# Low-order halves of some weight splits moved 32 bytes off a multiple of 64

## The chip, the cores and the metric

The kernel runs on one core of a Trainium2 chip. The metric is the device time of one execution in microseconds (us). TensorE does the matmuls, VectorE (DVE in the profile) and ScalarE (ACT) prepare weights and evacuate results, GpSimd (POOL) does small work and issues some DMAs, SyncE (SP) issues the weight DMAs. SBUF is the on-chip memory: 128 partitions, and an address in this text is a byte offset within a partition. PSUM holds the matmuls' sums.

## What is computed

A two-layer backbone over 256 latent tokens and 256 context tokens, width 1024. Each layer is an FFN, a mixing step with 16 attention heads of three kinds, and a second FFN, all pre-normed and modulated:

```python
for l in range(DEPTH):
    h = h + 0.5 * g1 * _swiglu(_modulate(_rms_norm(h, norm_ffn1[l]), sh1, sc1),
                               w_ffn1_gate[l], w_ffn1_up[l], w_ffn1_down[l])
    hc = hc + 0.5 * cg1 * _swiglu(...)              # same weights, context tokens
    p = u @ w_in[l]                                 # q, k, v of all heads
    ...
    h = h + gm * (jnp.concatenate([y_w, y_g, y_n], axis=-1) @ w_out[l])
    if not last: hc = hc + cgm * (yc @ w_out[l])
    h = h + 0.5 * g2 * _swiglu(...)
    if not last: hc = hc + 0.5 * cg2 * _swiglu(...)
```

The FFN's inner width is 2816. In the last layer the context tokens are needed only as keys and values, so its queries, output projection and second FFN run on the 256 latent tokens alone.

## The kernel before

Activations lie transposed: 128 channels on the partitions, 512 token columns (0 to 255 latent, 256 to 511 context). Weights come in chunks of 128 x 1024, one DMA each, into a `raw` buffer (three of them). To keep precision, each operand of a large matmul is split into a high part in the reduced type float32r and a low part that holds the rest: `wload` (L126) lets ACT copy the raw chunk to the high part (L129) and VectorE subtract it from the raw chunk for the low part (L130). Both parts lie in one `split` tile of 2 x 1024 elements, of which there are four buffers, 8192 bytes each: high part first, low part 4096 bytes on. The activations are split likewise (`Uh`, `Ul`, and `G` for the FFN's hidden tiles).

A product is then three matmuls per 128 x 128 weight block, in `mm3` (L133): high weight by high activation (L134), high weight by low activation (L135), low weight by high activation (L136). Each matmul instruction has its own weight load in the program that runs (PEld in the profile). A weight load reads 128 elements, 512 bytes per partition.

How many columns a matmul streams depends on the place. Where latent and context tokens run together it is 512. It is 256

- in the whole second FFN of layer 1 and in the queries and the output projection of layer 1 (latent tokens only);
- in the last of the four parts of `down` in each FFN and in the second part of the output projection, where latent and context tokens go one after the other, so that the next norm can begin (`piece`, `finish`);
- in the first two tiles of the second FFN of layer 0 and of the first of layer 1 (`up_two`), and in the first key and query chunks of a mixer, which also run per token half.

The order of the work around this is set by the program's order and the tile scheduler. `MIX` is a hand-written order of the mixer's steps, `START` one of the first tiles; neither is touched. A one-off tile named `fill` of 288 bytes stands ahead of the weight pool. With it, in the built program, `raw`, `split`, `H`, `Uh`, `Ul` and the `G` tiles all begin at multiples of 512 bytes: the four `split` buffers at 44544, 52736, 60928 and 69120.

Of the kernel before, what the change touches and what calls it, by code (L numbers as in the profile page):

```python
# [10 lines left out]
F32 = mybir.dt.float32  # L11
F32R = mybir.dt.float32r
AF = mybir.ActivationFunctionType
ALU = mybir.AluOpType
# [46 lines left out]
def hybrid_backbone(ctx: ExitStack, tc: tile.TileContext, I, out):  # L61
# [61 lines left out]
        nc.sync.dma_start(raw[:, :n], src)  # L123
        return raw

    def wload(src, n=1024):  # L126
        raw = raw_load(src, n)
        sp = wp.tile([128, 2, 1024], F32R, tag="split", name="split", bufs=4)
        act(sp[:, 0, :n], raw[:, :n], AF.Copy)  # L129
        tt(sp[:, 1, :n], raw[:, :n], sp[:, 0, :n].bitcast(F32), ALU.subtract)  # L130
        return sp

    def mm3(ps, wh, wl, xh, xl, first, last):  # L133
        mm(ps, wh, xh, start=first, stop=False)  # L134
# [3 lines left out]
    def proj(ps, sp, U, cols, nk=KT, off=0, k0=0, ks=None):  # L138
        for k in ks or range(nk):
            o = off + k * 128  # L140
            mm3(ps, sp[:, 0, o:o + 128], sp[:, 1, o:o + 128], U[0][:, k0 + k, cols], U[1][:, k0 + k, cols],
                k == 0, k == nk - 1)


# [116 lines left out]
    def first_tiles(pool, csel, U, src):  # L261

        pss, sps, rb, ada_ps, ada_pt, rstd, tmp = [], [], [], {}, {}, {}, {}

        def r(h):
            if not rb:
                rb.append(bank("o", "rb"))
            rstd[h] = norm_rstd_stages(h, rb[0], 256 * h, "mm")  # L270
            next(rstd[h])

        def s(h):
            next(rstd[h], None)

        def a(p, i):

            if i == 0:
                ada_ps[p] = bank("mm", "adaps")
            c, b = divmod(i, 2)  # L280
            raw = pool.tile([128, 4, 256], F32, tag="araw", name="araw", bufs=ABUFS)
            nc.sync.dma_start(raw, I["w_ada0"][:, p, c, b])
            for j in range(4):
                mm(ada_ps[p][32 * j:32 * j + 32, :256], csel[:, 2 * j + b, c, :], raw[:, j, :], start=(i == 0),
                   stop=(i == 3))

        def b(p):
            sb = pool.tile([128, 256], F32, tag="adasb", name="adasb", bufs=1)
            act(sb, ada_ps[p][:, :256], AF.Copy)
            pt = ada_pt[p] = bank("mm", "adapt")  # L290
            for i in range(2):
                nc.tensor.transpose(pt[:, i * 128:(i + 1) * 128], sb[:, i * 128:(i + 1) * 128], ident)

        def c(p):
            v = ada_pt[p][:, :256].rearrange("p (b j r) -> p b r j", b=2, j=4)
            for i in range(2):
                f = i * KT + 2 * p
                nc.vector.tensor_reduce(ada[0][:, f:f + 2, :], v[:, :, 2 * i:2 * i + 2, :], axis=AX.X, op=ALU.add)
            for m in ("sh1", "sc1"):
                ada_fin(0, m, 2, slice(2 * p, 2 * p + 2))  # L300

        def w(i):
            raw = raw_load(src(i), 1024)
            if i < 4:
                t = wp.tile([128, 2, 1024], F32R, tag="split", name="split", bufs=4)
                parts = [(t, 0, 1024)]
            else:
                parts = [(pool.tile([128, 2, 512], F32R, tag="G", name="split0", bufs=10), o, 512) for o in (0, 512)]
            for t, o, n in parts:
                act(t[:, 0, :], raw[:, o:o + n], AF.Copy)  # L310
            sps.append((raw, parts))

        def x(i):
            raw, parts = sps[i]
            for t, o, n in parts:
                tt(t[:, 1, :], raw[:, o:o + n], t[:, 0, :].bitcast(F32), ALU.subtract)
            pss.append(bank(("s", "t", "s", "t", "mm", "mm")[i], "pf"))

        def u(f):
            shv = mod(0, "sh1")  # L320
            t2 = pool.tile([128, 2, TOK], F32R, tag="G", name="t0", bufs=10)[:, 0, :].bitcast(F32)
            for h in range(2):
                cols = (LAT, CT)[h]
                t = tmp[f, h] = t2[:, cols]
                stt(t, H[:, f, cols], amod[0][:, 0, f, h:h + 1], rb[0][:, 256 * h:256 * h + 256], op0=ALU.mult,
                    op1=ALU.mult)
                marks["act"] = ins_of(act(U[0][:, f, cols], t, AF.Identity, bias=shv[:, f, h:h + 1]))

        def v(f):
            shv = mod(0, "sh1")  # L330
            for h in range(2):
                cols = (LAT, CT)[h]
                stt(U[1][:, f, cols], tmp.pop((f, h)), shv[:, f, h:h + 1], U[0][:, f, cols].bitcast(F32),
                    op0=ALU.add, op1=ALU.subtract)

        def m(i, f):
            t, o, _ = sps[i][1][f // 4 if i >= 4 else 0]
            wh, wl = (t[:, e, f * 128 - o:f * 128 - o + 128] for e in range(2))
            mm(pss[i], wh, U[0][:, f, :], start=(f == 0), stop=False)
            mm(pss[i], wl, U[0][:, f, :], start=False, stop=False)  # L340
            mm(pss[i], wh, U[1][:, f, :], start=False, stop=(f == KT - 1))

        steps = dict(r=r, s=s, a=a, b=b, c=c, w=w, x=x, u=u, v=v, m=m)
        with tc.manual_schedule():
            for o in START.split():
                steps[o[0]](*map(int, o[1:]))
        return pss


    def ffn(l, w, halves, pool, U, jobs, after, start=None):  # L350
# [12 lines left out]
                done += 1  # L363

        def chunk(src, ft):
            return wload(src[l, :, ft * 1024:(ft + 1) * 1024])

        def evac(pg, pu):
            g = pool.tile([128, 2, TOK], F32R, tag="G", name="G", bufs=10)
# [28 lines left out]
        def down(p0, n, last):  # L398
            if not last:
                for d in range(KT):  # L400
                    sp = wload(wd[l, :, off[0]:off[0] + n * 128], n * 128)
                    off[0] += n * 128
                    ps = bank("mm", "pd")
                    for k in range(n):
                        mm3(ps[:, cols], sp[:, 0, k * 128:k * 128 + 128], sp[:, 1, k * 128:k * 128 + 128],
                            G[p0 + k][:, 0, cols], G[p0 + k][:, 1, cols], k == 0, k == n - 1)
                    for h in halves:
                        accum(ps, h * 256, d, h, gate)
            else:
                sps = []  # L410
                for i in range(KT // 2):
                    sps.append(wload(wd[l, :, off[0]:off[0] + n * 256], n * 256))
                    off[0] += n * 256
                def piece(ps, d, h):
                    c = (LAT, CT)[h]
                    o = (d % 2) * n * 128
                    for k in range(n):
                        mm3(ps[:, :256], sps[d // 2][:, 0, o + k * 128:o + k * 128 + 128],
                            sps[d // 2][:, 1, o + k * 128:o + k * 128 + 128],
                            G[p0 + k][:, 0, c], G[p0 + k][:, 1, c], k == 0, k == n - 1)  # L420

                finish(halves, piece, gate, after)
# [30 lines left out]
    def mixer(l, pool, U):  # L453
# [5 lines left out]
            late[n] for n in ("perm", "rope", "maskA", "maskC", "hsel", "qkg", "sink", "nsink", "qg8"))  # L459

        def qk_chunk(i):
            return wload(win[l, :, i * 1024:(i + 1) * 1024])

        def rope_lat(x):
            sw = bank("mm", "sw")
# [109 lines left out]
        def v_tok(sps, nk, n, dst, t):  # L575
            ps = bank("mm", "pv")
            for k in range(KT):
                s, o = sps[k // nk], (k % nk) * n
                c = slice(t * 128, t * 128 + 128)
                mm(ps[:, :n], U[0][:, k, c], s[:, 0, o:o + n], start=(k == 0), stop=False)  # L580
                mm(ps[:, :n], U[0][:, k, c], s[:, 1, o:o + n], start=False, stop=False)
                mm(ps[:, :n], U[1][:, k, c], s[:, 0, o:o + n], start=False, stop=(k == KT - 1))
            p = ps[:, :n].rearrange("p (h d) -> p h d", d=64)
            act(dst[:, t, :, 0, :], p, AF.Copy)
            tt(dst[:, t, :, 1, :], p, dst[:, t, :, 0, :].bitcast(F32), ALU.subtract)
# [185 lines left out]
    def out_proj(l, halves, Y, qcols, after):  # L771
# [5 lines left out]
        for part in range(2):  # L777
            sps = []
            if part == 0:
                for d in range(KT):  # L780
                    if d % 2 == 0:
                        i = d // 2
                        sp = wload(I["w_out"][l, :, i * 1024:(i + 1) * 1024])
                    ps = bank("mm", "pd")
                    proj(ps[:, qcols], sp, Z, qcols, nk=4, off=(d % 2) * 512)
                    for h in halves:
                        accum(ps, h * 256, d, h, gate)
            else:
                sps = [wload(I["w_out"][l, :, (4 + i) * 1024:(5 + i) * 1024]) for i in range(4)]

                def piece(ps, d, h):
                    proj(ps[:, :256], sps[d // 2], Z, (LAT, CT)[h], nk=4, off=(d % 2) * 512, k0=4)

                finish(halves, piece, gate, after)
# [154 lines left out]
```

## Time and profile before

| what | us |
|---|---|
| median of three runs (1742.02 to 1744.09) | 1743.22 |
| the profiled execution's own time | 1742.45 |
| its span, first to last instruction | 1740.5 |
| TensorE (PE) busy, 9572 matmuls | 1700.8 |
| VectorE (DVE) busy | 1180.0 |
| ScalarE (ACT) busy | 718.5 |

The profiled execution is one run; its span leaves out 1.95 us at its ends. An engine's busy time is the union of its instructions. A matmul's recorded length contains its passage through the array, which overlaps the next matmul, so the distance between starts, not the length, is what a matmul costs in a dense stream.

### The profile page before, as it was taken

The page shows a single profiled execution, that of the slowest core. Times are in us where ns is not written, and L with a number is a line of the kernel's source. Part 1 is how long each engine was busy: PE and PEld are TensorE (multiplying, and loading weights), DVE is VectorE, ACT ScalarE, POOL GpSimd, SP SyncE. Part 2 cuts the span into 40 slices and gives each one's busy share as a digit, 9 for nine tenths or more (in the row PEclk, how much of TensorE's full clock was granted, in tenths as well). Part 3 has the DMA queues.
Part 4 walks back from the last instruction along what each step waited for, and adds up shares of the span by engine and source line. Part 5 has one row for each costly group of instructions (what it writes and reads, how often), then busy time and mean ns, then how long its engine had stood idle before and what let it go on. Part 6 is the DMA issues. An engine that isn't in the chain of part 4 may idle for free.

```text
span 1740.5 us, 24756 instructions
## 1 busy us (share of the span) xinstructions
PE 1700.8 (98%) x9572; PEld 1477.5 (85%) x9572; DVE 1180.0 (68%) x2031; ACT 718.5 (41%) x1206; POOL 165.8 (10%) x251
## 2 busy tenths in 40 slices
PE   7999999999999999999999999999999999989997
PEld 4888888889888898888888898888888888889997
DVE  5899963447978869983334599934343787965555
ACT  4322222235888653222222442222222577754443
POOL 0311100012102031100000212100000211100000
PEclk9999999999999999999999999999999999989999
DMA  8877643323223247743333288824332333356663
GB/s 330 309 240 243 197 117 84 110 73 115 58 82 85 75 169 238 236 129 89 108 85 109 63 319 277 321 79 115 85 109 86 99 84 102 109 155 182 182 176 113
DMA packets 76693, 258.37 MB, mean 148 GB/s; under 512 B 8944, under 2 KB 11248, under 8 KB 76192
## 3 DMA queue, kind: packets, MB, share of 16 engines
q1 hardware_dynamic: 54096, 176.72, 33.2%
q0 software_dynamic: 21760, 79.38, 14.3%
q8 instruction: 75, 1.23, 0.3%
q10 hardware_dynamic: 720, 0.69, 0.1%
q14 instruction: 42, 0.34, 0.1%
HBM read 250.47 MB, written 1.05 MB: 145 GB/s over the span
## 4 chain that ended last, share of the span: by engine, by line
PE 89%; DVE 4%; ACT 4%; issue 2%; POOL 1%; DMA 1%; POOLq 0%; DVEq 0%; SPq 0%; ACTq 0%
PE pd L135 8%; PE pd L134 8%; PE pd L136 8%; PE pu L134 8%; PE pu L135 8%; PE pu L136 8%; PE pg L134 8%; PE pg L136 8%; PE pg L135 8%; PE pq L136 1%; PE pq L134 1%; PE pq L135 1%; PE pt L679 1%; DVE split L130 1%; PE pv L580 1%
## 5 line engine op out<-in xcount | busy, mean ns | idle before, releaser
L129 ACT ACTIVATE split<-raw 128x1024 fp32r<-128x1024 f32 (+1 forms) x336 | 332.7, 991 | 546.6 <-PE pu L136 223.2
L130 DVE TENSOR_TENSOR split<-raw,split 128x1024 fp32r<-128x1024 f32 (+1 forms) x336 | 383.9, 1143 | 234.1 <-ACT split L129 233.2
L151 DVE SCALAR_TENSOR_TENSOR ascr<-araw,cb 128x1024 f32<-128x1024 f32 x224 | 273.3, 1220 | 9.9 <-ACT cb L804 7.0
L135 PE MATMUL pd<-G,split 128*128 128x512 f32 (+1 forms) x800 | 272.5, 341 | 0.0
L134 PE MATMUL pd<-G,split 128*128 128x512 f32 (+1 forms) x800 | 271.5, 341 | 0.0
L136 PE MATMUL pd<-G,split 128*128 128x512 f32 (+1 forms) x800 | 271.4, 340 | 0.0
L134 PE MATMUL pg<-Uh,split 128*128 128x512 f32 (+1 forms) x712 | 252.4, 355 | 2.1 <-ACT Uh L225 2.1
L136 PE MATMUL pg<-Uh,split 128*128 128x512 f32 (+1 forms) x712 | 252.3, 354 | 0.0
L135 PE MATMUL pg<-Ul,split 128*128 128x512 f32 (+1 forms) x712 | 252.0, 355 | 0.1
L134 PE MATMUL pu<-Uh,split 128*128 128x512 f32 (+1 forms) x712 | 252.1, 354 | 0.0
L135 PE MATMUL pu<-Ul,split 128*128 128x512 f32 (+1 forms) x712 | 251.9, 354 | 0.0
L136 PE MATMUL pu<-Uh,split 128*128 128x512 f32 (+1 forms) x712 | 251.9, 354 | 0.0
L234 DVE SCALAR_TENSOR_TENSOR H<-pd,ada,H 128x256 f32<-128x256 f32 x272 | 123.3, 479 | 106.9 <-PE pd L136 106.8
L135 PEld LDWEIGHTS pd<-G,split 128*128 128x128 f32 x800 | 151.6, 190 | 17.2
L136 PEld LDWEIGHTS pd<-G,split 128*128 128x128 f32 x800 | 151.4, 190 | 16.9
L134 PEld LDWEIGHTS pd<-G,split 128*128 128x128 f32 x800 | 151.1, 189 | 17.3
L134 PEld LDWEIGHTS pg<-Uh,split 128*128 128x128 f32 x712 | 135.4, 190 | 21.0 <-ACT Uh L225 2.6
L135 PEld LDWEIGHTS pg<-Ul,split 128*128 128x128 f32 x712 | 135.4, 190 | 18.6 <-DVE Ul L226 0.3
L136 PEld LDWEIGHTS pu<-Uh,split 128*128 128x128 f32 x712 | 135.2, 190 | 18.5
L136 PEld LDWEIGHTS pg<-Uh,split 128*128 128x128 f32 x712 | 135.2, 190 | 18.4
L134 PEld LDWEIGHTS pu<-Uh,split 128*128 128x128 f32 x712 | 135.3, 190 | 18.3
L135 PEld LDWEIGHTS pu<-Ul,split 128*128 128x128 f32 x712 | 135.0, 190 | 18.4
(199 smaller groups left out, 2412.6 us busy)
## 6 DMA issues: line engine op xcount, KB each, us to landing
araw<-in_w_adaT POOLq DMA_DIRECT2D x128, 512.0 KB, 5.0
raw<-in_w_ffn_gate SPq DMA_DIRECT2D x88, 512.0 KB, 3.8
raw<-in_w_ffn_up SPq DMA_DIRECT2D x88, 512.0 KB, 3.9
raw<-in_w_ffn_down SPq DMA_DIRECT2D x96, 384.0 KB, 3.2
raw<-in_w_in SPq DMA_DIRECT2D x26, 512.0 KB, 3.5
araw<-in_w_ada SPq DMA_DIRECT2D x16, 512.0 KB, 9.9
raw<-in_w_ffn_down SPq DMA_DIRECT2D x16, 512.0 KB, 3.6
raw<-in_w_out SPq DMA_DIRECT2D x16, 512.0 KB, 3.7
```

Of the source, the lines that this page charges most:

```text
L129: act(sp[:, 0, :n], raw[:, :n], AF.Copy)
L130: tt(sp[:, 1, :n], raw[:, :n], sp[:, 0, :n].bitcast(F32), ALU.subtract)
L134: mm(ps, wh, xh, start=first, stop=False)
L135: mm(ps, wh, xl, start=False, stop=False)
L136: mm(ps, wl, xh, start=False, stop=last)
L151: stt(scr, raw, 1.0, cb[:, t, :], op0=ALU.mult, op1=ALU.mult, accum_out=ada[l][:, ft, t:t + 1])
L234: stt(H[:, d, cols], ps[:, off:off + 256], gate[:, d, half:half + 1], H[:, d, cols], op0=ALU.mult, op1=ALU.add)
L580: mm(ps[:, :n], U[0][:, k, c], s[:, 0, o:o + n], start=(k == 0), stop=False)
L679: nc.tensor.transpose(pt[:, k * 128:(k + 1) * 128], P[t][:, k * 128:(k + 1) * 128], ident)
```

## The change

`halves_of` makes the split tile 2064 elements wide, 8256 bytes, and returns two views: the high part at 0, and the low part at element 1024, or at element 1032 where `pad` is set, 32 bytes further. `wload` returns the two views in place of one tile, and all users index them so. `pad` is set for the chunks of an FFN that runs on latent tokens alone, for the last part of `down` in every FFN, for the second part of both output projections and the first part of layer 1's, and for the query chunks of layer 1; not for the chunks of `up_two`, of the values, of keys, or of the first tiles.

```diff
+    def halves_of(pad):
+
+        t = wp.tile([128, 2064], F32R, tag="split", name="split", bufs=4)
+        o = 1024 + (8 if pad else 0)
+        return t[:, :1024], t[:, o:o + 1024]
+
-    def wload(src, n=1024):
+    def wload(src, n=1024, pad=False):
         raw = raw_load(src, n)
-        sp = wp.tile([128, 2, 1024], F32R, tag="split", name="split", bufs=4)
-        act(sp[:, 0, :n], raw[:, :n], AF.Copy)
-        tt(sp[:, 1, :n], raw[:, :n], sp[:, 0, :n].bitcast(F32), ALU.subtract)
-        return sp
+        hi, lo = halves_of(pad)
+        act(hi[:, :n], raw[:, :n], AF.Copy)
+        tt(lo[:, :n], raw[:, :n], hi[:, :n].bitcast(F32), ALU.subtract)
+        return hi, lo
...
         def chunk(src, ft):
-            return wload(src[l, :, ft * 1024:(ft + 1) * 1024])
+            return wload(src[l, :, ft * 1024:(ft + 1) * 1024], pad=not both)
...
-                    sp = wload(wd[l, :, off[0]:off[0] + n * 128], n * 128)
+                    sp = wload(wd[l, :, off[0]:off[0] + n * 128], n * 128, not both)
...
-                    sps.append(wload(wd[l, :, off[0]:off[0] + n * 256], n * 256))
+                    sps.append(wload(wd[l, :, off[0]:off[0] + n * 256], n * 256, True))
...
-            return wload(win[l, :, i * 1024:(i + 1) * 1024])
+            return wload(win[l, :, i * 1024:(i + 1) * 1024], pad=i < 8 and not ctxq)
...
-                        sp = wload(I["w_out"][l, :, i * 1024:(i + 1) * 1024])
+                        sp = wload(I["w_out"][l, :, i * 1024:(i + 1) * 1024], pad=len(halves) == 1)
...
-                sps = [wload(I["w_out"][l, :, (4 + i) * 1024:(5 + i) * 1024]) for i in range(4)]
+                sps = [wload(I["w_out"][l, :, (4 + i) * 1024:(5 + i) * 1024], pad=True) for i in range(4)]
```

In the built program the four `split` buffers then begin at 44544, 52800, 61056 and 69312, and what lies behind them moves by 256 bytes (`H` from 77312 to 77568). The instructions of every engine are the same in number, form, order and waits; line numbers from 126 on move.

## Rows read from the trace of the kernel before

**Rows 1.** The page's head and strips: span, busy shares, granted clock in tenths.

```profile
span 1740.5 us, 24756 instructions
...
PE 1700.8 (98%) x9572; PEld 1477.5 (85%) x9572; DVE 1180.0 (68%) x2031; ACT 718.5 (41%) x1206; POOL 165.8 (10%) x251
...
PEclk9999999999999999999999999999999999989999
```

**Rows 2.** The page's chain that ended last: shares of the span by engine.

```profile
PE 89%; DVE 4%; ACT 4%; issue 2%; POOL 1%; DMA 1%; POOLq 0%; DVEq 0%; SPq 0%; ACTq 0%
```

**Rows 3.** Groups by line and shape, one matmul line: count, busy us, mean ns.

```profile
L135 PE MATMUL pd<-G,split 128*128 128x256 f32 x368 | 104.4, 285 | 0.0
...
L135 PE MATMUL pg<-Ul,split 128*128 128x256 f32 x240 | 68.4, 287 | 0.1
...
L135 PE MATMUL pu<-Ul,split 128*128 128x256 f32 x240 | 68.3, 285 | 0.0
...
L135 PE MATMUL pd<-Ul,split 128*128 128x256 f32 x128 | 36.2, 285 | 0.0
...
L135 PE MATMUL pq<-Ul,split 128*128 128x256 f32 x80 | 22.7, 284 | 0.0
```

**Rows 4.** Busy time by stretch, two stretches without stalls (x is instructions).

```profile
core 0: us, PE busy (x) PEld busy (x) DVE busy (x) ACT busy (x) POOL busy (x), PEclk, DMA share, GB/s
700.00:900.00 200.00, 200.00 (x884) 165.60 (x883) 119.40 (x180) 52.46 (x66) 6.16 (x12) 1.00 0.44 130
1560.00:1720.00 160.00, 160.00 (x1335) 159.90 (x1333) 93.91 (x123) 71.44 (x100) 0.00 (x0) 1.00 0.62 179
```

**Rows 5.** TensorE's instructions in time after a break, layer 1's mixer: start, length.

```profile
1506.16 0.40 PE L630 MATMUL S<-kd,q 128*128 128x512 f32 x1
1506.39 0.28 PE L136 MATMUL pd<-Uh,split 128*128 128x256 f32 x1
1506.51 0.28 PE L134 MATMUL pd<-Uh,split 128*128 128x256 f32 x1
1506.63 0.28 PE L135 MATMUL pd<-Ul,split 128*128 128x256 f32 x1
1506.75 0.28 PE L136 MATMUL pd<-Uh,split 128*128 128x256 f32 x1
1506.87 0.28 PE L134 MATMUL pd<-Uh,split 128*128 128x256 f32 x1
1506.98 0.28 PE L135 MATMUL pd<-Ul,split 128*128 128x256 f32 x1
```

**Rows 6.** The same view after another break, layer 0's mixer, 512 columns.

```profile
510.36 0.48 PE L134 MATMUL pq<-Uh,split 128*128 128x512 f32 x1
510.68 0.40 PE L135 MATMUL pq<-Ul,split 128*128 128x512 f32 x1
510.92 0.39 PE L136 MATMUL pq<-Uh,split 128*128 128x512 f32 x1
511.15 0.40 PE L629 MATMUL S<-kd,q 128*128 128x512 f32 x1
511.38 0.40 PE L630 MATMUL S<-kd,q 128*128 128x512 f32 x1
511.62 0.27 PE L679 MATMUL pt<-ident,P 128*128 128x128 f32 x1
```

**Rows 7.** TensorE's weight loads in time, at a head's transposes.

```profile
1511.70 0.90 PEld L679 LDWEIGHTS pt<-ident,P 128*128 128x128 f32 x8
1512.56 0.19 PEld L136 LDWEIGHTS pd<-Uh,split 128*128 128x128 f32 x1
```

**Rows 8.** What ACT waited for in the last FFN: us, times, longest.

```profile
...
ACT split L129 <- PE pu L136: 29.9, 19, 1.7
...
ACT split L129 <- PE pd L136: 20.0, 16, 1.3
```

More of the change, by code (lines that the diff above doesn't have):

```diff
@@ L140, in proj @@
             o = off + k * 128
-            mm3(ps, sp[:, 0, o:o + 128], sp[:, 1, o:o + 128], U[0][:, k0 + k, cols], U[1][:, k0 + k, cols],
+            mm3(ps, sp[0][:, o:o + 128], sp[1][:, o:o + 128], U[0][:, k0 + k, cols], U[1][:, k0 + k, cols],
                 k == 0, k == nk - 1)
@@ L304, in w @@
             if i < 4:
-                t = wp.tile([128, 2, 1024], F32R, tag="split", name="split", bufs=4)
-                parts = [(t, 0, 1024)]
-            else:
-                parts = [(pool.tile([128, 2, 512], F32R, tag="G", name="split0", bufs=10), o, 512) for o in (0, 512)]
+                parts = [(halves_of(False), 0, 1024)]
+            else:
+                ts = [pool.tile([128, 2, 512], F32R, tag="G", name="split0", bufs=10) for _ in range(2)]
+                parts = [((t[:, 0], t[:, 1]), o, 512) for t, o in zip(ts, (0, 512))]
             for t, o, n in parts:
-                act(t[:, 0, :], raw[:, o:o + n], AF.Copy)
+                act(t[0], raw[:, o:o + n], AF.Copy)
             sps.append((raw, parts))
@@ L315, in x @@
             for t, o, n in parts:
-                tt(t[:, 1, :], raw[:, o:o + n], t[:, 0, :].bitcast(F32), ALU.subtract)
+                tt(t[1], raw[:, o:o + n], t[0].bitcast(F32), ALU.subtract)
             pss.append(bank(("s", "t", "s", "t", "mm", "mm")[i], "pf"))
@@ L337, in m @@
             t, o, _ = sps[i][1][f // 4 if i >= 4 else 0]
-            wh, wl = (t[:, e, f * 128 - o:f * 128 - o + 128] for e in range(2))
+            wh, wl = (t[e][:, f * 128 - o:f * 128 - o + 128] for e in range(2))
             mm(pss[i], wh, U[0][:, f, :], start=(f == 0), stop=False)
@@ L404, in down @@
                     for k in range(n):
-                        mm3(ps[:, cols], sp[:, 0, k * 128:k * 128 + 128], sp[:, 1, k * 128:k * 128 + 128],
+                        mm3(ps[:, cols], sp[0][:, k * 128:k * 128 + 128], sp[1][:, k * 128:k * 128 + 128],
                             G[p0 + k][:, 0, cols], G[p0 + k][:, 1, cols], k == 0, k == n - 1)
@@ L417, in piece @@
                     for k in range(n):
-                        mm3(ps[:, :256], sps[d // 2][:, 0, o + k * 128:o + k * 128 + 128],
-                            sps[d // 2][:, 1, o + k * 128:o + k * 128 + 128],
+                        mm3(ps[:, :256], sps[d // 2][0][:, o + k * 128:o + k * 128 + 128],
+                            sps[d // 2][1][:, o + k * 128:o + k * 128 + 128],
                             G[p0 + k][:, 0, c], G[p0 + k][:, 1, c], k == 0, k == n - 1)
@@ L579, in v_tok @@
                 c = slice(t * 128, t * 128 + 128)
-                mm(ps[:, :n], U[0][:, k, c], s[:, 0, o:o + n], start=(k == 0), stop=False)
-                mm(ps[:, :n], U[0][:, k, c], s[:, 1, o:o + n], start=False, stop=False)
-                mm(ps[:, :n], U[1][:, k, c], s[:, 0, o:o + n], start=False, stop=(k == KT - 1))
+                mm(ps[:, :n], U[0][:, k, c], s[0][:, o:o + n], start=(k == 0), stop=False)
+                mm(ps[:, :n], U[0][:, k, c], s[1][:, o:o + n], start=False, stop=False)
+                mm(ps[:, :n], U[1][:, k, c], s[0][:, o:o + n], start=False, stop=(k == KT - 1))
             p = ps[:, :n].rearrange("p (h d) -> p h d", d=64)
```

## The prediction

> **What bounds the kernel now.** I read the page's summary first: TensorE is busy for 98% of the span, and the strip of granted clock is at its highest digit in all slices but one [rows 1]. The chain that ended last is 89% TensorE [rows 2]. So the span is, almost everywhere, a stream of matmuls that follow one another, and what counts is the distance from one matmul's start to the next one's, not the "mean ns" of a row, which contains the drain that overlaps the next matmul: 285 ns for 256 columns [rows 3].
>
> That distance is read from a window without a stall. Between 1560 and 1720 us, inside the last FFN, only 256-column matmuls run, TensorE waits for nothing and the granted clock is 1.00 (the 2.4 GHz level): 1333 weight loads in 160.00 us, 120.0 ns each [rows 4]. Between 700 and 900 us only 512-column matmuls run: 883 in 200.00 us, 226.5 ns each [rows 4]. The 256 extra columns cost 106.5 ns, so the columns alone of a 256-column matmul take about 106.5 ns and every matmul, long or short, carries some 13.5 ns beside them. That share is the only thing in a matmul's time that an address could change, since the columns, the bytes and the instruction count stay.
>
> Is the share fixed? Two places in the trace say that it isn't. Just after a change of work in the mixer of layer 1, 256-column matmuls start at 1506.39, .51, .63, .75, .87 and .98: five distances in 0.59 us, 118 ns each [rows 5]. The same form then settles at 120.0. After a similar break 512-column matmuls start at 510.68, .92, 511.15, .38 and .62: four in 0.94 us, 235 ns each, and they settle at 226.5 [rows 6]. So for one and the same shape the distance depends on how the weight load and the running matmul lie against each other, and the steady stream has settled into one such position: 2 ns slower than the unsettled one at 256 columns, 8.5 ns faster at 512. This is the argument on which I rest the forecast.
>
> **The change part by part.** The instructions of every engine stand in the same order as before, with the same waits; only line numbers and addresses move. In the built program of before, each operand of a split matmul starts at a multiple of 512 bytes. After, four things differ.
>
> (1) In the padded splits the low part starts 32 bytes past a multiple of 64. The number of weight loads that read it is counted from the loops and agrees with the rows: the last FFN has 22 x 8 for the gate, as many for up, and as many for down; the last part of down of the other three FFNs 8 x 4 x 2 each; the output projection 64 + 32 + 32; the query chunks of layer 1 64. Against the trace's 256-column groups of one of the three matmul lines, 368, 240, 240, 128 and 80 [rows 3], that is all of down and of the output projection, and all but 64 gate, 64 up and 16 query matmuls that belong to unpadded splits: 368 + 176 + 176 + 128 + 64 = 912. Each stands in a triple with two high-part loads, so 912 triples, 2736 matmuls, 328 us of the span at 120.0 ns.
>
> What one triple gains isn't in the trace, because no weight load of before lies off the 64-byte raster. The bounds come from the nearest rows. Upwards: the transposes, whose weight loads follow each other without a long stream beside them, run 8 loads in 0.86 us (1511.70 to the next load at 1512.56), 108 ns each [rows 7]; no weight load in the trace is faster. If the shifted low loads alone fell from 120.0 to 108, the gain is 912 x 12 = 10.9 us; if all three of a triple did, 2736 x 12 = 32.8 us. Downwards: a low load might pay a second share of 13.5 ns, 912 x 13.5 = 12.3 us of loss. Between the ends I take the row that is nearest, the same shape with the settled position broken [rows 5]: two of three loads in a triple now change from one raster to the other, so the stream should be thrown out of its settled position again and again and run near 118 instead of 120. 2736 x 2.0 = 5.5 us of gain.
>
> Of this, everything lies on the path: TensorE has no wait in the window. The cover for the faster stream is there: per 24 matmuls (2.88 us) one chunk needs an ACT copy and a VectorE subtract, and over the 160 us VectorE is busy 93.91 and ACT 71.44 us with the DMA engines at 0.62 [rows 4]; the ACT copies wait for TensorE to free a split buffer, 29.9 and 20.0 us in total [rows 8]. At 118 ns this slack shrinks by 2% and stays.
>
> (2) The rest of the splits keep their low part at 4096 bytes, so nothing in their own layout changes. (3) A split buffer grows from 8192 to 8256 bytes, so the four buffers start 0, 64, 128 and 192 bytes past a multiple of 256, and what lies behind them moves by 256 bytes. All stay multiples of 64, so no unpadded load moves against the 64-byte raster, and I cost this at nothing; its price, if it matters, is in the rivals. (4) VectorE writes the low part at the new address. If that took longer, VectorE's idle 41% of the window covers it [rows 4].
>
> **A rule against it.** The Trainium skill's page "SBUF — State Buffer", section "Specifications (TRN2)", gives the memory lines of 16 bytes, and its section "Who interferes with whom" gives TensorE two independent read ports, one for the streamed operand and one for weight loads. By these a shift of 32 bytes, two whole lines, changes nothing: 1743.2 us. The trace shows a distance that varies at the same addresses [rows 5], which independent ports alone would not give; but no run so far moves an address, so the rule stays as a rival.
>
> **The rivals.** *Nothing comes of the address* (the case of that rule): the settled position is one of clocks or of the array, not of SBUF addresses, the pad is invisible, and the time is 1743.2. For it: lines 134, 135 and 136, with differing operands, all settle at the same value. Against it: nothing but the analogy of an unsettled stream.
>
> *The low load pays more* (slower): the shifted load straddles the raster, reads one piece more, and takes its matmul a second 13.5 ns: 912 of them, +12.3 us, 1755.5. It decides from the point where a shifted load costs more than 2736 x 2.0 / 912 = 6 ns over what the broken position gives back. For it: the break made 512-column matmuls slower by 8.5 ns [rows 6], so a disturbed position can cost. Against it: at 256 columns the disturbed position was the faster one [rows 5].
>
> *The gain is given back by the others*: the new starts of the four buffers unsettle the 512-column stream at each new chunk. Four matmuls at 235 instead of 226.5 are 34 ns; the loops hold 209 chunks that stream 512 columns: +7.1 us against -5.5, so 1744.8, inside what can't be told from no change.
>
> *The low loads become free of the conflict*: -10.9 us, 1732.3, to -32.8 us if whole triples do, 1710.4.
>
> **How the numbers follow.** The profiled execution took 1742.45 us, 1.95 more than its span of 1740.5, and lies 0.77 under the median of three, 1743.22. The sum: 1742.45 - 5.5 = 1736.95 for an execution like it, or 1743.22 - 5.5 = 1737.7 against the median, which I give. Chances: forecast 0.48; free of the conflict 0.10; nothing 0.20; given back 0.06; slower 0.16. About 0.2%, 3.5 us, is what a measurement of this kernel can tell from no change; so faster than 1739.7 has 0.58, within 0.26, slower 0.16. The range leaves out the slower rival and the larger part of the conflict-free one: from 1726, a gain of 17 us, between the low loads' whole 10.9 and the triples' 32.8, to 1746.5, the upper edge of no change. The likeliest case's own range, 117 to 118.7 ns per matmul, is 1735.0 to 1739.7.
>
> **What would show it.** In the profile of the changed kernel, the window of the last FFN without stalls: more than 1333 weight loads in 160 us, 1356 if 118 ns is right, 1333 if nothing comes of it, 1285 if the low load pays 13.5 ns. Which of the three distances moved says more: low load after high, or all. The 512-column window must stay at 883 loads in 200 us; fewer means the new buffer starts cost. The mean ns of the copy and the subtract should stay. I am wrong if the distance at 256 columns doesn't move, or if it moves and the span doesn't follow by 2736 times as much.

## Result, and the profile after

| | median, us | lowest to highest, us | runs | ratio to before |
|---|---|---|---|---|
| before | 1742.62 | 1741.89 to 1744.09 | 4 | |
| after | 1755.44 | 1753.56 to 1756.27 | 4 | 1.0071 [1.0054, 1.0088] |

The change made the kernel slower by 12.8 us, where 5.5 us of gain was forecast; the time lies above the predicted range. The profiled execution of after took 1755.47 us, its span 1753.5, 13.0 more than that of before [rows 1]. Its page begins like this (span, busy us with share and instructions, granted clock in tenths over 40 slices):

```profile
span 1753.5 us, 24756 instructions
...
PE 1713.5 (98%) x9572; PEld 1472.7 (84%) x9572; DVE 1181.8 (67%) x2031; ACT 717.8 (41%) x1206; POOL 166.5 (9%) x251
...
PEclk9999999999999999999999999999999999999999
```

TensorE's busy time grew by 12.7 us (1700.8 to 1713.5) with the same 9572 matmuls, and VectorE's, ScalarE's and GpSimd's moved by at most 1.8. No new wait carries the loss, and the clock strip is no lower than before: the matmuls themselves follow each other more slowly. Which ones, the two windows without stalls tell (busy time by stretch, x is instructions; the second window lies 10 us later than in [rows 4] since the last FFN begins later):

```profile
core 0: us, PE busy (x) PEld busy (x) DVE busy (x) ACT busy (x) POOL busy (x), PEclk, DMA share, GB/s
700.00:900.00 200.00, 200.00 (x868) 162.97 (x868) 124.40 (x188) 52.12 (x66) 7.39 (x14) 1.00 0.46 136
1570.00:1730.00 160.00, 160.00 (x1358) 160.00 (x1357) 95.58 (x126) 72.63 (x101) 0.00 (x0) 1.00 0.65 188
```

In the 256-column window there are now 1357 weight loads in 160 us where there were 1333 [rows 4]: 117.9 ns each, not 120.0. In the 512-column window there are 868 in 200 us where there were 883: 230.4 ns each, not 226.5. So the gain is there, 2.1 ns per short matmul, and a loss of 3.9 ns on each long one, which the change was not meant to touch. The granted clock is 1.00 in both.

The groups by line and shape show that the loss lies on all long matmuls alike (count, busy us, mean ns of one). First one group of before, with 512 columns:

```profile
L134 PE MATMUL pg<-Uh,split 128*128 128x512 f32 x472 | 183.6, 389 | 0.0
```

Then groups of after, lines 140 to 142 being the three matmuls of `mm3`:

```profile
L140 PE MATMUL pg<-Uh,split 128*128 128x512 f32 x472 | 185.7, 393 | 0.0
...
L141 PE MATMUL pu<-Ul,split 128*128 128x512 f32 x472 | 185.1, 392 | 0.0
...
L141 PE MATMUL pd<-G,split 128*128 128x512 f32 x432 | 169.6, 393 | 0.0
L141 PE MATMUL pd<-G,split 128*128 128x256 f32 x368 | 103.5, 283 | 0.0
```

High and low weights, gate, up and down: all went from 389 to between 392 and 394 ns, while the 256-column group fell from 285 [rows 3] to 283. One matmul line has 472 + 472 + 432 + 120 (queries) + 32 (output projection) = 1528 matmuls with 512 columns, three lines 4584, and the first tiles 144 more: 4728 x 3.9 = +18.4 us. The 256-column matmuls of split weights are 3 x (368 + 240 + 240 + 128 + 80) = 3168 [rows 3] and 96 for keys: 3264 x 2.1 = -6.9 us. The sum is +11.5 of the span's 13.0. Of the rest 1.2 us stands in two waits of TensorE (total us, times, longest), before:

```profile
PE ss L201 <- DVE acc L193: 11.9, 3, 9.5
...
PE pv L581 <- DVE split L130: 0.8, 2, 0.5
```

and after:

```profile
PE ss L207 <- DVE acc L199: 12.2, 3, 9.9
...
PE pv L588 <- DVE split L136: 1.7, 2, 0.9
```

Where does the loss come from? None of these chunks is padded; only their buffers' starts have moved. TensorE's matmuls in time, at the first matmul of five successive chunks in the second FFN of layer 0 (start us, length us):

```profile
694.31 0.39 PE L140 MATMUL pg<-Uh,split 128*128 128x512 f32 x1
...
699.81 0.39 PE L140 MATMUL pu<-Uh,split 128*128 128x512 f32 x1
...
705.27 0.40 PE L140 MATMUL pg<-Uh,split 128*128 128x512 f32 x1
...
710.86 0.39 PE L140 MATMUL pu<-Uh,split 128*128 128x512 f32 x1
...
716.45 0.39 PE L140 MATMUL pd<-G,split 128*128 128x512 f32 x1
```

A chunk is 8 blocks, 24 matmuls. In the built program these four chunks lie in the buffers at 69312, 44544, 61056 and 52800, which are 192, 0, 128 and 64 bytes past a multiple of 256; the streamed `Uh` begins at a multiple of 256. They take 5.50, 5.46, 5.59 and 5.59 us: 229, 227, 233 and 233 ns per matmul. The chunk whose buffer didn't move against 256 keeps the distance of before, and the other three lose 2 to 6 ns.

### The profile page after: what moved, and what is told of

It reads as the page before. It is cut to its first block, busy times and chain, and to the rows that moved or that the text cites. A ratio compares the mean times of both kernels' runs of the same rounds, so it can differ in the third digit from the quotient of the medians.

```text
span 1753.5 us, 24756 instructions
## 1 busy us (share of the span) xinstructions
PE 1713.5 (98%) x9572; PEld 1472.7 (84%) x9572; DVE 1181.8 (67%) x2031; ACT 717.8 (41%) x1206; POOL 166.5 (9%) x251
## 4 chain that ended last, share of the span: by engine, by line
PE 89%; DVE 3%; ACT 3%; issue 2%; POOL 1%; DMA 1%; POOLq 0%; SPq 0%; DVEq 0%; ACTq 0%
PE pd L141 9%; PE pd L142 8%; PE pd L140 8%; PE pu L142 8%; PE pu L140 8%; PE pu L141 8%; PE pg L140 8%; PE pg L142 8%; PE pg L141 8%; PE pq L142 1%; PE pq L140 1%; PE pq L141 1%; PE pt L686 1%; PE pv L587 1%; PE pv L588 1%
## 5 line engine op out<-in xcount | busy, mean ns | idle before, releaser
L141 PE MATMUL pd<-G,split 128*128 128x512 f32 (+1 forms) x800 | 273.2, 342 | 0.0
L142 PE MATMUL pd<-G,split 128*128 128x512 f32 (+1 forms) x800 | 272.9, 342 | 0.0
L140 PE MATMUL pd<-G,split 128*128 128x512 f32 (+1 forms) x800 | 272.2, 342 | 0.0
L140 PE MATMUL pg<-Uh,split 128*128 128x512 f32 (+1 forms) x712 | 253.7, 357 | 2.1 <-ACT Uh L231 2.1
L142 PE MATMUL pg<-Uh,split 128*128 128x512 f32 (+1 forms) x712 | 253.7, 356 | 0.0
L142 PE MATMUL pu<-Uh,split 128*128 128x512 f32 (+1 forms) x712 | 253.3, 356 | 0.0
L140 PE MATMUL pu<-Uh,split 128*128 128x512 f32 (+1 forms) x712 | 253.2, 356 | 0.0
L141 PE MATMUL pu<-Ul,split 128*128 128x512 f32 (+1 forms) x712 | 252.8, 355 | 0.0
L141 PE MATMUL pg<-Ul,split 128*128 128x512 f32 (+1 forms) x712 | 252.4, 355 | 0.1
L141 PEld LDWEIGHTS pd<-G,split 128*128 128x128 f32 x800 | 150.5, 188 | 19.2
L140 PEld LDWEIGHTS pd<-G,split 128*128 128x128 f32 x800 | 150.1, 188 | 18.8
L142 PEld LDWEIGHTS pd<-G,split 128*128 128x128 f32 x800 | 150.3, 188 | 18.4
L140 PEld LDWEIGHTS pg<-Uh,split 128*128 128x128 f32 x712 | 134.5, 189 | 22.3 <-ACT Uh L231 2.6
L141 PEld LDWEIGHTS pg<-Ul,split 128*128 128x128 f32 x712 | 134.3, 189 | 20.6 <-DVE Ul L232 0.3
L142 PEld LDWEIGHTS pg<-Uh,split 128*128 128x128 f32 x712 | 134.3, 189 | 20.4
L142 PEld LDWEIGHTS pu<-Uh,split 128*128 128x128 f32 x712 | 134.2, 189 | 20.4
L141 PEld LDWEIGHTS pu<-Ul,split 128*128 128x128 f32 x712 | 134.2, 189 | 20.3
L140 PEld LDWEIGHTS pu<-Uh,split 128*128 128x128 f32 x712 | 134.6, 189 | 19.8
```

The source lines that it names most:

```text
L141: mm(ps, wh, xl, start=False, stop=False)
L142: mm(ps, wl, xh, start=False, stop=last)
```

## The experiments

The kernel before ran beside each group of experiments: median 1742.58 us with e1 to e4, 1742.24 with e5, e6, e7 and e9, 1742.35 with e10 and e11; ratios are against these. The comparison leaves three things to tell apart: whether the 32-byte shift or the new buffer starts (theory S) made each of the two differences; whether what counts is where the weights lie absolutely, or where they lie against the streamed activations (theory R); and what each start costs.

**e1: the buffer size alone.** The tile keeps its 8256 bytes, the low part goes back to 4096 bytes behind the high part, everywhere:

```diff
-        o = 1024 + (8 if pad else 0)
+        o = 1024
```

> The changed kernel without its shift: the split tile stays 8256 bytes, so the four buffers start 0, 64, 128 and 192 bytes past a multiple of 256, but every low part lies 4096 bytes behind its high part. Theory S (the buffers' new starts did the harm, and at 256 columns the good too): 512-column matmuls stay at about 230.8 ns apart and 256-column ones at about 117.5, as in the changed kernel, so the time stays at 1755, within 3 us. Theory P (the 32-byte shift gives the gain at 256 columns, the buffers' starts cost at 512): 256 columns go back to 120.0 and the time to 1755.4 + 5.5 = 1761. Theory Q (the shift itself did the harm by unsettling the stream): the time goes back to 1742.6.

Measured: 1753.88 us (1753.40 to 1756.57), ratio 1.0070 [1.0054, 1.0087]. Its windows (columns as above):

```profile
700.00:900.00 200.00, 200.00 (x869) 162.97 (x868) 121.16 (x182) 51.33 (x64) 6.89 (x13) 1.00 0.45 131
1570.00:1730.00 160.00, 160.00 (x1359) 159.90 (x1358) 96.43 (x127) 72.97 (x102) 0.00 (x0) 1.00 0.63 185
```

868 and 1358 loads, the same as after within a load. Both differences, the gain too, come from the starts of the buffers; beside them the shift that the change is about adds nothing that can be measured.

**e2: the activations moved, the weights not.** In the kernel before, a 64-byte tile between the weight pool and the activations moves everything behind the weights by 64 bytes:

```diff
+    gapp = ep(tc.tile_pool(name="gap", bufs=1))
+    gapp.tile([128, 64], mybir.dt.uint8, name="gap")
```

> The kernel before with a hole of 64 bytes between the weight buffers and everything behind them: all weight parts start at multiples of 512, all activations 64 bytes past one. Theory R (what counts is where the weight load starts against where the stream starts): the weights now lie 192 past the stream modulo 256, so 512 columns go from 226.8 to about 229.3 ns and 256 columns from 120.0 to about 117, some +12 and -9 us: 1745, and both distances move. Theory A (the weight's own address counts): nothing moves, 1742.6, 226.8 and 120.0.

Measured: 1746.45 us (1742.83 to 1753.38), ratio 1.0031 [1.0015, 1.0046]. The two windows, and between them one in the first FFN of layer 1, where 512 columns run too:

```profile
700.00:900.00 200.00, 200.00 (x859) 162.00 (x858) 118.08 (x177) 51.33 (x64) 6.36 (x12) 1.00 0.43 127
1100.00:1300.00 200.00, 200.00 (x875) 164.11 (x874) 99.81 (x146) 51.51 (x65) 7.42 (x14) 1.00 0.43 139
1560.00:1720.00 160.00, 160.00 (x1360) 160.00 (x1360) 96.99 (x127) 73.19 (x102) 0.00 (x0) 1.00 0.66 191
```

No weight moved, and yet 512 columns go to 233.1 ns in the first of these windows and 256 columns to 117.6. In layer 1's first FFN the same form, with the same starts of weights and stream, takes 228.8 ns (874 loads in 200 us). So one start has two steady distances here, 4.3 ns apart, each kept throughout its window; a loss of 6.6 ns on all 4728 would be 31 us. The runs of this kernel are spread over 10.6 us, and its profiled execution, 1750.61 us, lies in the upper part; whether the shorter runs had more stretches at 228.8, no profile here shows.

**e3: both moved together.** In the kernel before, the `fill` tile ahead of all of them grows by 64 bytes:

```diff
-FILL = 288
+FILL = 352
```

> The kernel before with its one-off tile of 288 bytes made 352, so that weights and activations alike start 64 bytes past a multiple of 512. Theory R (relative starts): nothing moves, 226.8 and 120.0 ns, 1742.6. Theory A (the weight's own address): all 512-column matmuls go to the 233 ns that the changed kernel shows for its buffer at 64, some +29 us, and 256 columns to 117, -9 us: about 1762.

Measured: 1742.79 us (1741.45 to 1743.98), ratio 1.0001 [0.9992, 1.0010].

```profile
700.00:900.00 200.00, 200.00 (x884) 165.62 (x883) 120.84 (x182) 51.98 (x65) 6.36 (x12) 1.00 0.45 133
1560.00:1720.00 160.00, 160.00 (x1333) 159.86 (x1333) 94.72 (x126) 70.22 (x98) 0.00 (x0) 1.00 0.61 178
```

883 and 1333, as in [rows 4] to the load. Every operand is now 64 bytes off its old raster, and nothing changed. So it is the start of the weights against the stream that counts. The Trainium skill's page "SBUF — State Buffer", section "Who interferes with whom", gives TensorE two independent read ports, one for the stream and one for weight loads, and says that TensorE and ScalarE never wait on anyone. By these neither e2 nor e3 should have changed anything. In e3 nothing changed; e2 moved only what the one port reads, and the distances changed by 6.6 and 2.4 ns. Whether it is the two reads that meet, or something behind them, no run here tells.

**e4: what each start costs.** A kernel of bare streams, without the backbone: no DMA, no chunks, triples of matmuls as in `mm3`, 144 in a row for each case. `w` is the byte offset of all weights against a multiple of 256, `lo` that of the low part alone, `x` that of the stream:

```python
for n, w, lo, x in CONFIGS:
    ...
    for t in range(total):
        k = t % 8
        o = w // 4 + k * 128
        wh, wl = W[:, o:o + 128], W[:, 1024 + lo // 4 + o:1152 + lo // 4 + o]
        c = k * 512 + x // 4
        xh = xf[:, c:c + n]
        ...
        for i, (wt, mv) in enumerate(((wh, xh), (wh, xl), (wl, xh))):
            mm(ps[:, :n], wt, mv, ...)
```

> No backbone at all: only streams of 144 matmuls of one kind, one stream after another, in triples as in the kernel (high weight by high stream, high by low, low by high), eight weight blocks in turn, no other engine at work. A stream's name gives its columns (n), the byte offset of both weight parts (w), a further offset of the low part (lo) or of the moving operand (x). Theory R: at 512 columns 226.7 ns per matmul at offset 0, about 233 at 64 and 128, about 229 at 192, and the streams with weights and moving operand shifted alike as at 0; at 256 columns 120 at offset 0 and 117 to 118 elsewhere. Theory A: the streams with only the moving operand shifted stay at 226.7 and 120. Of the low part alone shifted by 32 at 256 columns: about 118 if the shift gives the gain, 120 if it doesn't. If another engine's traffic and not the address is at work, all streams of a length are alike.

Groups by name, longest first (count, busy us, mean ns); the distance is the busy time less one mean, over 143:

```profile
L153 PE MATMUL n512w0x64b<-X,W 128*128 128x512 f32 x144 | 33.8, 397 | 0.0
...
L153 PE MATMUL n512w64lo0b<-X,W 128*128 128x512 f32 x144 | 33.8, 395 | 0.0
...
L153 PE MATMUL n512w0lo32b<-X,W 128*128 128x512 f32 x144 | 33.8, 395 | 0.0
L153 PE MATMUL n512w128lo0b<-X,W 128*128 128x512 f32 x144 | 33.6, 394 | 0.0
...
L153 PE MATMUL n512w192lo0b<-X,W 128*128 128x512 f32 x144 | 33.1, 391 | 0.0
...
L153 PE MATMUL n512w64x64b<-X,W 128*128 128x512 f32 x144 | 32.8, 389 | 0.0
...
L153 PE MATMUL n512w0lo0b<-X,W 128*128 128x512 f32 x144 | 32.8, 389 | 0.0
...
L153 PE MATMUL n256w0lo0b<-X,W 128*128 128x256 f32 x144 | 17.4, 283 | 0.0
...
L153 PE MATMUL n256w0lo32b<-X,W 128*128 128x256 f32 x144 | 17.2, 281 | 0.0
...
L153 PE MATMUL n256w8lo0b<-X,W 128*128 128x256 f32 x144 | 16.8, 278 | 0.0
L153 PE MATMUL n256w64lo0b<-X,W 128*128 128x256 f32 x144 | 16.5, 276 | 0.0
L153 PE MATMUL n256w0x192b<-X,W 128*128 128x256 f32 x144 | 16.5, 276 | 0.0
```

The bare stream gives the kernel's own distances. From the starts of the single matmuls, 512 columns take 226.7 ns at 0, 233.3 at 64, 232.4 at 128 and 228.9 at 192: within 1 ns the 227, 233, 233 and 229 of the four buffers of after. 256 columns take 120.0, 113.3, 118.6 and 117.8. Weights and stream moved together by 64 give 226.7 and 120.0, the values at 0; the stream moved by 192 gives 113.3, like the weights moved by 64. One pair seems not to fit a plain difference: with 512 columns the stream moved by 64 takes 233.3, the weights moved by 192 228.9. But the weights of e2 lie 192 past the stream too, and in one execution they ran at both distances, so these are two steady distances of one start. The change's own idea, low part moved by 32 (`lo32`), gains 1.7 ns with 256 columns (118.3) and costs 6.6 with 512 (233.3).

**e5 and e6: the change without its side effect.** Each `split` buffer is 8448 bytes (33 x 256), so that all four start at a multiple of 256; to make room, `fill` shrinks and two scratch tiles of the rotary step move into buffers of the norm. e5 is the control, without the shift:

```diff
-FILL = 288
+FILL = 32
...
-        t = wp.tile([128, 2064], F32R, tag="split", name="split", bufs=4)
-        o = 1024 + (8 if pad else 0)
+        t = wp.tile([128, 2112], F32R, tag="split", name="split", bufs=4)
+        o = 1024
...
-            a = pool.tile([128, 256], F32, tag="ra", name="ra", bufs=1)
-            b = pool.tile([128, 256], F32, tag="rb_", name="rb_", bufs=1)
+            a = npl.tile([128, 256], F32, tag="t", name="ra", bufs=2)
+            b = npl.tile([128, 256], F32, tag="sq", name="rb_", bufs=2)
```

> The changed kernel without its shift, with a split tile of 8448 bytes (33 x 256) in place of 8256, so that all four buffers and everything behind them start at multiples of 256; the room comes from a smaller one-off tile and from two scratch tiles of the rotation that now use idle buffers of the norm pool. The control for the next three. If the buffers' starts modulo 256 did the harm: 226.7 and 120.0 ns as before, 1742.6 us within 3. If a larger tile or the moved scratch costs by itself: above 1746.

e6 has the same edits and keeps the change's line for `o`:

```diff
-        o = 1024
+        o = 1024 + (8 if pad else 0)
```

> The change as it was described, with the harm of the buffers' starts taken out: buffers of 8448 bytes as in the control, and the low part 32 bytes further in the same 912 x 128 columns of low weights as in the changed kernel. By the sweep (256 columns, low part at 32: 118.3 ns; offset 0: 120.0) 2736 matmuls gain 1.7 ns, 4.6 us: 1738.0, with the 512-column distance at 226.7. By the forecast's 118 it is 5.5 us: 1737. If the shift gives nothing in the kernel: 1742.6.

Measured: e5 1743.50 us (1741.42 to 1745.57), ratio 1.0009 [0.9999, 1.0018]; e6 1739.90 us (1738.78 to 1741.55), ratio 0.9987 [0.9977, 0.9996]. The windows of e5:

```profile
700.00:900.00 200.00, 200.00 (x884) 165.62 (x883) 119.91 (x182) 52.23 (x66) 6.36 (x12) 1.00 0.45 131
1560.00:1720.00 160.00, 160.00 (x1334) 159.89 (x1332) 94.73 (x124) 70.65 (x99) 0.00 (x0) 1.00 0.61 179
```

and of e6:

```profile
700.00:900.00 200.00, 200.00 (x884) 165.66 (x883) 118.83 (x180) 52.69 (x67) 5.83 (x11) 1.00 0.44 129
1560.00:1720.00 160.00, 160.00 (x1352) 159.84 (x1351) 95.83 (x127) 71.31 (x102) 0.44 (x1) 1.00 0.62 179
```

Buffers that start at a multiple of 256 bring back 883 loads in the 512-column window, whatever their size. The shift alone brings 1351 loads in the other, 118.4 ns: 2736 x 1.6 = 4.4 us by the window, 3.6 against the control and 2.3 against before by the medians. That is the change that was predicted; it gains 2.3 to 4.4 us where 5.5 was forecast.

**e7 and e9: the fastest start of the sweep.** With the buffers of e5, both parts of a padded split move by 64 bytes (113.3 ns in e4, which on 2736 matmuls would be 18 us):

```diff
-        o = 1024 + (8 if pad else 0)
-        return t[:, :1024], t[:, o:o + 1024]
+        o = 16 if pad else 0
+        return t[:, o:o + 1024], t[:, o + 1024:o + 2048]
```

> The same buffers and the same splits, but in those splits both the high and the low part start 64 bytes past a multiple of 256. By the sweep (256 columns, both at 64: 113.3 ns) 2736 matmuls gain 6.7 ns, 18.2 us: 1724.4, with the 512-column distance unchanged. If the kernel's other traffic blurs the position, the gain shrinks to that of any offset, 2 ns each: 1737. If weight preparation or DMA can't follow the faster stream, TensorE shows waits in the last FFN and the gain stops between.

e9 does the same also for the chunks of `up_two` and the first key and query chunks, so for all 3264:

```diff
-        def chunk(src, ft):
-            return wload(src[l, :, ft * 1024:(ft + 1) * 1024], pad=not both)
+        def chunk(src, ft, pad=False):
+            return wload(src[l, :, ft * 1024:(ft + 1) * 1024], pad=pad or not both)
...
-                sps += [chunk(wg, ft + i), chunk(wu, ft + i)]
+                sps += [chunk(wg, ft + i, True), chunk(wu, ft + i, True)]
...
-            return wload(win[l, :, i * 1024:(i + 1) * 1024], pad=i < 8 and not ctxq)
+            return wload(win[l, :, i * 1024:(i + 1) * 1024], pad=i in (0, 8) or (i < 8 and not ctxq))
```

> As the run with both parts at 64, and the same shift in the other splits whose matmuls all stream 256 columns: the two first tiles of two FFNs and the first key and query chunk of each mixer, 3264 matmuls instead of 2736. 3264 x 6.7 = 21.8 us less than before: 1720.8. If the extra ones sit beside waits, as part of the mixer's do, between 1721 and 1724.

Measured: e7 1733.08 us (1731.18 to 1740.52), ratio 0.9953 [0.9942, 0.9964]; e9 1732.02 us (1729.11 to 1740.55), ratio 0.9949 [0.9934, 0.9963]. Both are faster than before and after, but e7 by 9.2 us against before, half of the 18. The window of e7:

```profile
1560.00:1700.00 140.00, 140.00 (x1191) 140.00 (x1191) 84.45 (x113) 63.23 (x88) 0.00 (x0) 1.00 0.64 188
```

Two windows of e9, one in the first tiles of layer 1's first FFN and one in the last FFN:

```profile
1003.60:1021.60 18.00, 18.00 (x159) 17.96 (x158) 15.14 (x27) 9.51 (x14) 1.63 (x4) 1.00 0.96 382
1545.00:1700.00 155.00, 155.00 (x1318) 155.00 (x1317) 93.25 (x123) 71.72 (x101) 0.00 (x0) 1.00 0.63 184
```

At the same offset the stream runs at 113.9 ns in one stretch (158 loads in 18.00 us) and at 117.7 in the other, in one execution. There are two steady positions, as in e2, and the long stretch fell into the slower one. For e7 the window gives 2736 x 2.4 = 6.6 us; the medians give 9.2 against before and 10.4 against the control e5. The profiled executions of e7 and e9 are the longest of their runs; whether the shorter ones had more stretches at 113.3, no profile here shows.

**e8 and e11: a finer sweep, and what picks the position.** e8 is the sweep of e4 with other offsets:

```python
for n, w, lo, x in CONFIGS:    # w: 4, 12, 20, ... 320; with 256, 384 and 512 columns
```

> A second set of the bare streams, at finer offsets of the weights against the moving operand, no backbone. What repeats modulo 256: if only the start modulo 256 counts, w256 reads as w0 (120.0 at 256 columns, 226.7 at 512) and w320 as w64 (113.3). Where the best position ends: w60 and w68 at 113.3 if 16 bytes either way make no difference, 117 to 118 if the position is exact. Whether some offset at 512 columns is faster than 226.7: none is expected, the columns alone take 213.

Some of its groups (columns as for e4):

```profile
L142 PE MATMUL n512w320lo0b<-X,W 128*128 128x512 f32 x144 | 33.8, 396 | 0.0
...
L142 PE MATMUL n512w256lo0b<-X,W 128*128 128x512 f32 x144 | 32.8, 389 | 0.0
...
L142 PE MATMUL n256w256lo0b<-X,W 128*128 128x256 f32 x144 | 17.4, 283 | 0.0
...
L142 PE MATMUL n256w320lo0b<-X,W 128*128 128x256 f32 x144 | 17.1, 281 | 0.0
...
L142 PE MATMUL n256w64lo0b<-X,W 128*128 128x256 f32 x144 | 16.5, 276 | 0.0
```

256 is as 0, with both shapes. No offset brings 512 columns below the 226.7 ns of the kernel before, and none brings 256 below 113.3; the dearest is 121.8 at 24. At 320 the 512-column stream is as at 64, the 256-column one is not (117.8, not 113.3). e11 asks whether that is the offset or what ran ahead: each case follows 48 matmuls of another one, named behind `after`:

```python
for n, w, name in CONFIGS:     # a "pre" case of 48 matmuls, then 144 of the measured case
    total = 48 if name[0] == "n" else 16
```

> Bare streams again, no backbone: 256 columns with both weight parts at 64, at 256 + 64 or at 8, each entered from nine different short streams (the name tells which). If offset 64 has two settled positions and the way of entering picks one, some of its nine streams read 113.3 and others 117.8, and 320 behaves as 64 does. If 64 and 320 differ by themselves, all nine of 64 read 113.3 and all nine of 320 read 117.8. Offset 8: 115.6 in all nine if it has one position.

```profile
L153 PE MATMUL n256w320after256w0x<-X,W 128*128 128x256 f32 x144 | 17.1, 281 | 0.0
L153 PE MATMUL n256w64after256w0x<-X,W 128*128 128x256 f32 x144 | 17.1, 281 | 0.0
...
L153 PE MATMUL n256w8after256w0x<-X,W 128*128 128x256 f32 x144 | 16.8, 278 | 0.0
...
L153 PE MATMUL n256w64after256w56x<-X,W 128*128 128x256 f32 x144 | 16.5, 276 | 0.0
...
L153 PE MATMUL n256w320after256w192x<-X,W 128*128 128x256 f32 x144 | 16.5, 276 | 0.0
```

64 and 320 behave alike, so the period of 256 stands, and both have two positions: 113.3 ns after 256 columns at 56, 96 or 192, and 117.8 after 256 at 0 or 48, 384 at 0 and 512 at 0, 64 or 192. What runs ahead picks the position, and 144 matmuls later the stream is still in it. In the profiled executions of e7 and e9 the last FFN is in the slower one. At 8 the distance is 115.6 after all nine. The offsets of e4 and e8 were each entered from one stream only, in one execution, so any value there may be one of two.

**e10: the offset with one position.** e9 with 8 bytes in place of 64:

```diff
-        o = 16 if pad else 0
+        o = 2 if pad else 0
```

> As the run with 3264 shifted matmuls, but both parts start 8 bytes past a multiple of 256 instead of 64. The sweeps gave 115.6 ns at 8 both times, entered from different streams, while 64 gave 113.3 and 256 + 64 gave 117.8. If 64 has two settled positions and 8 only one, the kernel runs its 256-column stream at 115.6: 3264 x 4.4 = 14.4 us less than before, 1728. If the kernel's stream settles at 8 as it does at 64, near 117: 1732 to 1733.

Measured: 1733.56 us (1732.84 to 1734.50), ratio 0.9946 [0.9929, 0.9963]. A window, and the longest wait of TensorE (total us, times, longest):

```profile
1560.00:1700.00 140.00, 140.00 (x1214) 140.00 (x1214) 85.49 (x115) 64.93 (x90) 0.00 (x0) 1.00 0.66 191
```

```profile
PE ss L207 <- DVE acc L199: 13.5, 3, 9.7
```

1214 loads in 140 us, 115.3 ns: the position holds, and its runs lie within 1.7 us of each other, where e9's lie within 11.4. But 3264 x 4.7 = 15.3 us by the window became 8.8 by the medians. The wait of the norm's column sum for VectorE, 11.9 us before, took back 1.6; that fits a TensorE that comes earlier and waits longer for the same accumulation. Pairing the matmuls of the two traces, the gain stays in the last FFN, where the lead over before grows from 2.3 to 8.2 us; ahead of it most was given back where TensorE doesn't run densely, and why there, no run here tells.

## Why the prediction was wrong, point by point

- **What bounds the kernel** was right: the loss stands in the distance between matmuls, and TensorE stayed busy for 98% of the span.
- **Step (1), the gain.** The distance fell to 117.9 where 118 was forecast, and the window holds 1357 loads where 1356 were named. That agreement is luck: in the changed kernel the buffer starts make the gain (e1), and the shift alone, in e6, brings 118.4. The way that it was to come about, a stream thrown out of its settled position again and again, isn't what the bare stream shows either: with the low part at 32 (e4) the distances repeat every 12 matmuls, between 115 and 121 ns, to the end of the stream, so this is a steady position too. What was right is that one and the same form has more than one distance, by how weights and stream lie against each other. The prediction asked which of a triple's three distances moves: all do, in e6's window from 120.0 to 118.8, 117.4 and 119.2 ns before L141, L142 and L140.
- **Step (3) failed.** "All stay multiples of 64, so no unpadded load moves against the 64-byte raster, and I cost this at nothing". There is no raster of that kind: e3 moved everything by 64 at no cost, and e2 moved only the stream and changed both distances. What counts is the start of the weights against the stream (256 bytes on it is as at 0, and 320 as at 64), and three of the four buffers had left the start at which 512 columns take 226.7 ns. The step was worth +18.4 us.
- **The bound was in the rows.** [rows 6] shows 512 columns at 235 ns in a disturbed position, 8.5 more than in the steady one. The prediction saw that the steady position was the good one for 512 columns and the bad one for 256, and then let the change touch the good one at no price. 4728 x 8.5 = 40 us was the upper bound of step (3), and it belonged in the range.
- **Given back by the others** was the right kind of rival, mis-sized: it took four matmuls at each chunk's start, 34 ns per chunk and 7.1 us in all. The stream doesn't recover within a chunk: the chunks above take 5.59 us in place of 24 x 226.5 ns = 5.44, 150 ns more, from the first matmul to the last.
- **The low load pays more** named 1755.5 us, and 1755.44 was measured. It is refuted all the same: it needs 1285 loads in the 256-column window, and 1357 are there; e1 takes the shifted low loads away and stays at 1753.88. A time that fits shows no mechanism; the observable written beside it did.
- **Nothing comes of the address** is refuted by e1, e2 and e6. **Free of the conflict** got nowhere near its 108 ns: no start of the sweeps is below 113.3. That no weight load is faster than those of [rows 7] holds for 128 columns at most: the loads for `adaps` (L284), 32 columns wide, run 8 in 0.20 us.
- **Step (2)** held in that the parts of an unpadded split still lie 4096 bytes apart, and it didn't help them. **Step (4)** shows no cost: VectorE's busy time rose by 1.8 us in 1180, and TensorE's waits by the 1.2 named above.
- **What would show it** served: "883 loads in 200 us; fewer means the new buffer starts cost" is what happened, at 868.

## What to carry to other kernels

A tile's size is an address for all that is allocated behind it and for the next buffer of the same tile: when an edit grows a rotating buffer, price the new starts for every stream that uses it, not only for the one that the edit is about. Where a trace shows one shape at two steady distances, ask which shapes sit in the good position now, and keep them there (here: buffer sizes in multiples of 256 bytes) while moving only the others. Judge such an edit by the number of weight loads in windows without stalls, for each shape and in more than one stage, since one start can have two distances, and hold a rival to its observable before its time.

## What the runs showed of the hardware

- With these 128 x 128 float32r weight loads ahead of every matmul, the steady distance depends on the weights' start against the stream's: 113.3 to 121.8 ns with 256 columns, 226.7 to 234.3 with 512. 384 columns are affected less (173.5 at 0, 176.7 at 64). The best start for one shape is not that for another: 64 bytes is the fastest for 256 columns, and costs 6.6 ns with 512.
- The Trainium skill's page "TensorE: Matmul & The Clock Gate", section "Back-to-back issue gap", gives 262 cycles for an isolated matmul of 256 columns and 518 for one of 512, which at 2.4 GHz are 109 and 216 ns (an estimate from its figures), and a sustained 131 ns for 512. Every steady stream of these shapes here stays above them, at 113.3 and 226.7 ns or more; for these operands the measurement decides.
- A start can have two steady positions: with 256 columns at 64 they are 113.3 and 117.8 ns, picked by what ran ahead and kept for at least 144 matmuls (e11); with 512 columns at 192 they are 228.8 and 233.1, each throughout a window of 200 us (e2), and what picks it there wasn't tried. What inside the chip makes the period of 256 bytes and the two positions was not found.
